# Two load queues, a reordered first stage and a longer warm-up in a two-layer mixer trunk

## The chip, the cores and the metric

The kernel runs on 1 core of one Trainium2 chip. The metric is device time in microseconds for one execution, as the median of the runs. Engines are named as in the profile: PE is TensorE's matmuls, PEld its weight loads, DVE is VectorE, ACT is ScalarE, POOL is GpSimd, SP issues DMAs.

## The reference

Two layers, each with one norm, one wide projection, four head groups and one output projection; a last norm ends it. x is 512 tokens by 1024, float32.

```python
def hybrid_layer(x, norm_w, w_in, w_out, ...):
    h = rmsnorm(x, norm_w)                 # x * rsqrt(mean(x^2) + eps) * norm_w
    p = split_cols(h @ w_in)               # 1024 by 3380 columns for four mixers
    o_a = dsa_mixer(...)   # indexer, top-128 keys of each query, attention
    o_b = nsa_mixer(...)   # compressed, selected and window attention, gated
    o_c = shortconv_mixer(...)
    o_d = pool_mixer(...)
    mixed = concat([silu(gate) * o for each group])
    return x + mixed @ w_out
```

## The kernel before

Tokens lie in four tiles of 128 (`NT`), the model width in eight chunks of 128 (`KC`). Each float32 factor of a projection is held as two float32r parts, high and low, and a product is three matmuls: L137 high by high, L138 low weights, L139 low activations, over eight chunks (24 matmuls of 360 columns for a tile of the first group).

`load_w` loads a group of columns of `w_in` by four quarters of its rows (two chunks each), casts a quarter to `wh` (for the first group on VectorE, L120) and subtracts to get `wl` (`lo`, L95; for the first group quarters 0 and 2 on GpSimd, 1 and 3 on VectorE). `first_loads(h)` puts the other first loads between these quarters. All DMAs of the first stage are issued by SP; at most eight are under way, since the ninth waits for the first one's landing.

The norm of a tile (`norm_tile`) works on two halves of 512 columns: ScalarE squares and sums (`junk`, L222), GpSimd adds the halves and takes the power -1/2 (L223, L234), VectorE multiplies x by the scale and by the norm's weights `g` (L237, `xn`), TensorE transposes four blocks (L246), ScalarE copies the high part of `hT` out of PSUM (L248), VectorE writes the low part (L95 `hT`). A tile's first matmul, L137, needs the high part; L139 needs the low part. After the 24 matmuls of a tile come the copies and the rotation of queries and keys, and four transposes (L385 and L386).

`g` is the norm's weight row, the same on all 128 partitions. Before the first norm TensorE runs 28 transposes of the identity on nothing (`WARM`). A scheduler fixes the order of instructions on each engine at build time; engines take their instructions in that order and wait on semaphores.

Of the kernel before, what the change touches and what calls it, by code (L numbers as in the profile page):

```python
# [17 lines left out]
P = 128  # L18
T = 512
# [8 lines left out]
TOPK = 128  # L28
BIG = 10  # places for tiles of [P, T]
WARM = 28  # products on nothing at the start  # L30
NEG = -1.0e30
MARK = -3.0e38
EPS = 1.0e-6

# first columns of the parts of w_in
A_Q, A_V, A_QI, A_KI, A_GATE, B_Q, B_KC, B_KS, B_GATE, C_B, C_GATE = 0, 320, 384, 640, 680, 936, 1192, 1320, 1588, 1844, 2612

# columns of the table of shape constants
TB64, TB32, TBC, TBN, TBW, TBL = 0, 128, 192, 224, 256, 258
# [26 lines left out]
def trunk(ctx: ExitStack, tc: tile.TileContext, x, norm_w, w_in, w_out, conv_w, pe_cmp, w_cmp_k, w_cmp_v,  # L66
# [26 lines left out]
    def lo(eng, dst, src, hi):  # L93
        """dst = src - hi, the part of src that its rounding to float32r left out."""
        eng.tensor_sub(dst, src, f(hi))  # L95

# [1 line left out]
    def load_w(src, segs, early=None, start=False):  # L98
        """segs: (first column, columns) runs of src that make up one group; by quarters of its rows.
        early: tag of a place that is still free for the loads; start: the first group of all"""  # L100
        n = sum(c for _, c in segs)
        parts = []
        stage = res.tile([P, KC, 384], F32, name=nm("ws"), tag=early) if early else None
        for h in range(4):
            if early:
                st = stage[:, 2 * h : 2 * h + 2, :]
            else:
                st = wp.tile([P, 2, 384], F32, name=nm("st"), tag="st", bufs=4)
            o = 0
            for c0, c in segs:  # L110
                nc.sync.dma_start(
                    st[:, :, o : o + c],
                    src[h * 256 : (h + 1) * 256, c0 : c0 + c].rearrange("(k p) c -> p k c", p=P))
                o += c
            if start:
                first_loads(h)
            wh = wp.tile([P, 2, 384], F32R, name=nm("wh"), tag="wh", bufs=6)
            wl = wp.tile([P, 2, 384], F32R, name=nm("wl"), tag="wl", bufs=6)
            if start:
                V.tensor_copy(wh[:, :, :n], st[:, :, :n])  # L120
            else:
                S.activation(wh[:, :, :n], st[:, :, :n], AF.Copy)  # L122
            lo(V if start and h % 2 else G, wl[:, :, :n], st[:, :, :n], wh[:, :, :n])
            parts.append((wh, wl))
        return parts
# [3 lines left out]
    def lin_tok(ps, act, i, w, c0, n, order=range(KC)):  # L129
        """ps[:, :n] = act (tokens of tile i) @ w[:, c0:c0+n]"""  # L130
        ts = slice(i * P, (i + 1) * P)
        order = list(order)
        for k in order:
            wh, wl = w[k // 2]
            rh, rl = wh[:, k % 2, c0 : c0 + n], wl[:, k % 2, c0 : c0 + n]
            st, sp = k == order[0], k == order[-1]
            PE.matmul(ps[:, :n], act[0][:, k, ts], rh, start=st, stop=False)  # L137
            PE.matmul(ps[:, :n], act[0][:, k, ts], rl, start=False, stop=False)  # L138
            PE.matmul(ps[:, :n], act[1][:, k, ts], rh, start=False, stop=sp)  # L139

    def lin_ch(act, w, c0):
        """(w[:, c0:c0+128])^T @ act^T : 128 channels by all tokens"""
        ps = bank("mm", 2)
        for k in range(KC):
            wh, wl = w[k // 2]
            lh, ll = wh[:, k % 2, c0 : c0 + P], wl[:, k % 2, c0 : c0 + P]
            PE.matmul(ps, lh, act[0][:, k, :], start=k == 0, stop=False)  # L147
            PE.matmul(ps, lh, act[1][:, k, :], start=False, stop=False)  # L148
            PE.matmul(ps, ll, act[0][:, k, :], start=False, stop=k == KC - 1)  # L149
        return ps  # L150

# [1 line left out]
    def half(b):  # L153
# [5 lines left out]
    def load_x(xt, src, i):  # L159
        for b in range(2):  # L160
            nc.sync.dma_start(xt[b], src[i * P : (i + 1) * P, half(b)])
# [7 lines left out]
    xt0 = [x_tile() for _ in range(NT)]  # L169
    load_x(xt0[0], x, 0)  # L170
    g_first = load_g(nc.sync, norm_w[0:1, :])
    ident = const.tile([P, P], F32, name="ident")
    make_identity(nc, ident)
    # the tensor engine's clock rises only after some microseconds of work: done on nothing while the loads run
    idle = bank("ms", 1)
    for _ in range(WARM):
        PE.transpose(idle[:, :P], ident, ident)
    tab = const.tile([P, TBL], F32, name="tab")
    mask = const.tile([P, T], F32, name="mask")
# [11 lines left out]
    def first_loads(h):  # L191
        """the other loads, between those of the first group of weights"""
        if h:
            load_x(xt0[h], x, h)
        if h == 1:
            nc.sync.dma_start(tab, table)
        if h == 3:
            G.memset(mask, 0.0)
# [19 lines left out]
    def mean_sq(xp, acc):  # L218
        """acc (EPS to begin with) and the part of the mean of squares that the columns xp make up"""
        junk = wk.tile([P, T], BF16, name=nm("junk"), tag="acc", bufs=3)  # L220
# [8 lines left out]
    def rms(xt, g, ms=None):  # L229
        """xt, g: by halves of the columns; ms: mean of xt's squares"""  # L230
        if ms is None:
# [20 lines left out]
    def rope(eng, z, n, half, tb, rows=P):  # L252
        """z: [rows, n, d], rotated in place; tb: [rows, 4*half] = cos, cos, -sin, sin"""
        r = 2 * half
# [12 lines left out]
    def pipeline(tasks, depth=4):  # L267
        """Starts a task with each round, and takes each of those under way a step further."""
        active = []
# [16 lines left out]
    def layer(l, hT, w_first, norm):  # L286
        """hT: the layer's normalized input, transposed, w_first: its first group of weights; norm, if any, writes
        the tiles of hT. Returns the like for the next layer."""
        xsrc = x if l == 0 else x1d
# [5 lines left out]

# [1 line left out]
        kiT = res.tile([P, T], F32R, name=nm("kiT"), tag="kiT")  # L297
# [3 lines left out]
        def group_idx(i, w):  # L301
            """indexer queries of tile i, and the scores of its tokens against those before"""
            ps = bank("mm", 2)
# [6 lines left out]
            yield  # L310
            # rows of qiT[h % 4]: high, high, low part of the queries; of kiT: high, low, high part of the keys
            pq = bank("tr", 2)
# [31 lines left out]

# [1 line left out]
        qT = {}  # L346
        kTA = [res.tile([P, T], F32R, name=nm("kTA"), tag=f"kTA{s}") for s in range(2)]
        vA = res.tile([P, NT, P], F32R, name=nm("vA"), tag="vA")
        # keys of the selected and of the window branch; the compressed ones stand before the latter
        kTB = [res.tile([P, 2, 32 + T], F32R, name=nm("kTB"), tag=f"kTB{s}") for s in range(2)]  # L350
# [3 lines left out]
        def stack_q(m, i, pq):  # L354
            """pq: two heads a transpose; even heads as (high, low), odd ones as (low, high) rows"""
            q = wk.tile([P, NH, P], F32R, name=nm("q" + m), tag="q" + m, bufs=NT)
# [60 lines left out]
        def group_bq(i, w):  # L417
            """queries of the second mixer, values of the first"""
            ps = bank("mm", 2)
# [13 lines left out]

# [1 line left out]
        kcT = [kTB[s][:, 1, 0:32] for s in range(2)]  # L435
# [47 lines left out]

# [1 line left out]
        sg = {}  # L485

        def gates(m, j, w, c0):
            """tanh form of silu, twice its value: x (1 + tanh(x / 2))"""
            ps = lin_ch(hT, w, c0)
# [5 lines left out]
        def probs(m, i, kT, bias, gcol, cmp=None):  # L495
            """softmax over the keys of tiles 0..i; cmp: takes the scores of the 32 compressed keys, which stand
            before the others in kT"""
            n = P * (i + 1)
            c = 32 if cmp else 0
            per = T // n if n <= T // 2 else 1  # heads to a tile  # L500
            per = min(per, 2)
# [35 lines left out]
        def finish(m, i, po, c0):  # L537
            """adds the two halves of po, gates, and splits the result into the mixed activations"""
            ob = wk.tile([HD, T], F32, name=nm("ob"), tag="rl", bufs=2)
# [58 lines left out]

# [1 line left out]
        def cd(s="cd"):  # L600
# [63 lines left out]

# [1 line left out]
        def norm_a(i, w):  # L666
# [124 lines left out]
```

## Time and profile before

| | |
|---|---|
| median of 3 runs | 576.3 us (573.21, 576.3, 577.37) |
| profiled execution, span | 577.7 us, mean granted TensorE clock 0.971 |
| PE busy | 542.4 us, 94% of the span |
| VectorE, ScalarE, GpSimd busy | 448.9, 318.3, 296.0 us |
| DMA | 51.14 MB, mean 89 GB/s |

The profiled execution is one further execution. Its own time is given by its span, from the first to the last instruction, and is 1.4 us above the median of the runs. In the rows of a timeline the columns are start, duration, engine, line, operation, output and inputs by the program's names, and in brackets how long the engine stood idle ahead of it and what ended that. A row of a table by windows has the window, its length, then busy time of PE, PEld, DVE, ACT and POOL with counts, the granted clock, the DMA share and GB/s. A row of a group has a count, the busy time and the mean of one in ns.

### The profile page before, as it was taken

Reading aid. Unit: us, or ns where it says so; the run is one execution under the profiler, and the core shown is the slowest. Engines: PE = TensorE matmul, PEld = TensorE weight load, DVE = VectorE, ACT = ScalarE, POOL = GpSimd, SP = SyncE. Lnnn points to the kernel's source line nnn. Section 1 sums busy time; section 2 is a strip of 40 time slices with the busy share of each in tenths; the row PEclk is TensorE's granted clock in tenths of the full one; section 3 lists DMA queues with packets and bytes.
Section 4 is the critical chain, followed back from the end, with each engine's and each line's share of the span. In section 5 each row is a group of like instructions: output and inputs, shape, how many; then the busy total and the mean of one; then the engine's idle time right before and its main releaser. Section 6 shows DMA issues by size and latency. Waiting matters only on the chain.

```text
span 577.7 us, 9703 instructions
## 1 busy us (share of the span) xinstructions
PE 542.4 (94%) x3088; PEld 473.1 (82%) x3088; DVE 448.9 (78%) x1154; ACT 318.3 (55%) x787; POOL 296.0 (51%) x394
## 2 busy tenths in 40 slices
PE   5989799798999999999999989989999999999995
PEld 4989697676878877699999978768788887869895
DVE  4867899799999977762275769987999997897523
ACT  3457855253547566663455595536454756565433
POOL 4755641364546194643675455326554639273342
PEclk9899999799999999999999999987999999999999
DMA  8632311283222020526531512116513212123303
GB/s 260 192 94 54 74 34 23 56 209 83 54 56 65 28 79 13 147 91 198 147 117 48 141 35 64 37 37 178 134 30 81 64 48 58 52 88 114 111 1 145
DMA packets 70370, 51.14 MB, mean 89 GB/s; under 512 B 19248, under 2 KB 64432, under 8 KB 70320
## 3 DMA queue, kind: packets, MB, share of 16 engines
q1 hardware_dynamic: 70320, 50.54, 31.8%
q8 instruction: 24, 0.39, 0.3%
q14 instruction: 26, 0.21, 0.1%
HBM read 46.33 MB, written 4.19 MB: 87 GB/s over the span
## 4 chain that ended last, share of the span: by engine, by line
PE 67%; DVE 22%; ACT 4%; POOL 2%; issue 2%; DMA 2%; SPq 1%; POOLq 0%; ACTq 0%; DVEq 0%
PE mm L139 9%; PE mm L137 9%; PE mm L138 8%; PE mm L147 7%; PE mm L148 7%; PE mm L149 7%; PE tr L529 4%; DVE acc L342 4%; DVE acc L331 4%; DVE m L341 3%; PE ms L467 2%; PE s L509 2%; PE s L510 2%; PE pv L535 2%; PE pv L534 2%
## 5 line engine op out<-in xcount | busy, mean ns | idle before, releaser
L95 POOL TENSOR_TENSOR wl<-st,wh 128x768 fp32r<-128x768 f32 (+4 forms) x94 | 159.2, 1713 | 63.2 <-ACT wh L122 51.2
L147 PE MATMUL mm<-hT,wh 128*128 128x512 f32 x272 | 110.1, 405 | 3.8 <-DVE sg L493 3.0
L149 PE MATMUL mm<-hT,wl 128*128 128x512 f32 x272 | 108.2, 399 | 0.0
L148 PE MATMUL mm<-hT,wh 128*128 128x512 f32 x272 | 108.1, 399 | 0.0
L522 POOL TENSOR_SCALAR pb<-pb,rs 128x512 f32<-128x512 f32 (+3 forms) x96 | 53.7, 577 | 98.8 <-DVE rs L519 39.0
L515 ACT ACTIVATE pb<-pb,mn 128x512 f32<-128x512 f32 (+3 forms) x96 | 53.7, 559 | 72.1 <-DVE mn L513 71.6
L122 ACT ACTIVATE wh<-st 128x768 fp32r<-128x768 f32 (+4 forms) x92 | 70.7, 775 | 25.4 <-DMA st<-in_w_in_dram 9.2
L137 PE MATMUL mm<-wh,hT 128*128 128x360 f32 (+3 forms) x240 | 74.8, 313 | 8.1 <-ACT hT L248 4.3
L139 PE MATMUL mm<-wh,hT 128*128 128x360 f32 (+3 forms) x240 | 74.7, 312 | 0.9 <-DVE hT L95 0.9
L138 PE MATMUL mm<-wl,hT 128*128 128x360 f32 (+3 forms) x240 | 74.1, 310 | 0.0
L147 PEld LDWEIGHTS mm<-hT,wh 128*128 128x128 f32 x272 | 51.8, 191 | 14.2 <-DVE sg L493 3.5
L137 PE MATMUL mm<-wh,mT 128*128 128x384 f32 (+1 forms) x192 | 61.7, 323 | 0.3 <-ACT mT L604 0.3
L139 PE MATMUL mm<-wh,mT 128*128 128x384 f32 (+1 forms) x192 | 61.1, 320 | 0.6 <-DVE mT L95 0.6
L138 PE MATMUL mm<-wl,mT 128*128 128x384 f32 (+1 forms) x192 | 61.4, 320 | 0.0
L148 PEld LDWEIGHTS mm<-hT,wh 128*128 128x128 f32 x272 | 51.9, 191 | 9.7 <-issue 0.4
L149 PEld LDWEIGHTS mm<-hT,wl 128*128 128x128 f32 x272 | 51.4, 189 | 10.1 <-issue 0.5
L95 DVE TENSOR_TENSOR pl<-tr,ph 128x512 fp32r<-128x512 f32 (+1 forms) x68 | 45.9, 681 | 15.3 <-ACT ph L532 14.0
L137 PEld LDWEIGHTS mm<-wh,hT 128*128 128x128 f32 x240 | 46.1, 193 | 9.7 <-ACT hT L248 4.8
L341 DVE MAX8 m<-acc 128x8 f32<-128x384 f32 (+2 forms) x96 | 52.1, 552 | 0.4
L342 DVE MATCH_REPLACE8 acc<-m,acc 128x384 f32<-128x384 f32 (+2 forms) x96 | 52.0, 543 | 0.1
L139 PEld LDWEIGHTS mm<-wh,hT 128*128 128x128 f32 x240 | 46.1, 192 | 1.7 <-DVE hT L95 1.7
L138 PEld LDWEIGHTS mm<-wl,hT 128*128 128x128 f32 x240 | 46.2, 193 | 0.2
(194 smaller groups left out, 1171.5 us busy)
## 6 DMA issues: line engine op xcount, KB each, us to landing
st<-in_w_in_dram SPq DMA_DIRECT2D x104, 128.0 KB, 2.8
st<-in_w_in_dram SPq DMA_DIRECT2D x28, 256.0 KB, 3.0
st<-in_w_out_dram SPq DMA_DIRECT2D x16, 384.0 KB, 3.3
x<-in_x_dram SPq DMA_DIRECT2D x16, 256.0 KB, 4.1
st<-in_w_in_dram SPq DMA_DIRECT2D x8, 320.0 KB, 4.8
st<-in_w_out_dram SPq DMA_DIRECT2D x8, 256.0 KB, 3.0
x1d<-x SPq DMA_DIRECT2D x8, 256.0 KB, 2.4
x<-x1d SPq DMA_DIRECT2D x8, 256.0 KB, 3.3
```

What stands on the lines that cost most here:

```text
L95: eng.tensor_sub(dst, src, f(hi))
L122: S.activation(wh[:, :, :n], st[:, :, :n], AF.Copy)
L137: PE.matmul(ps[:, :n], act[0][:, k, ts], rh, start=st, stop=False)
L138: PE.matmul(ps[:, :n], act[0][:, k, ts], rl, start=False, stop=False)
L139: PE.matmul(ps[:, :n], act[1][:, k, ts], rh, start=False, stop=sp)
L147: PE.matmul(ps, lh, act[0][:, k, :], start=k == 0, stop=False)
L148: PE.matmul(ps, lh, act[1][:, k, :], start=False, stop=False)
L149: PE.matmul(ps, ll, act[0][:, k, :], start=False, stop=k == KC - 1)
L341: V.max(m8, a)
L342: V.match_replace(a, m8, a, MARK)
L515: S.activation(p, p, AF.Exp, scale=-1.0, bias=mn[:, h : h + 1], accum_out=rs[:, h : h + 1])
L522: G.tensor_scalar(p, p, rs[:, h : h + 1], 0.0, op0=OP.mult, op1=OP.add)
```

## The change

Four edits, all ahead of the first layer's projections:

- x tile 0 and the norm's weights are loaded by ScalarE's queue, the weights as one row of 4 KB (`grow`) and not as two broadcasts of 256 KB to all partitions. SP starts at once with the first group of weights.
- x tiles 1 to 3 and the table come behind all four quarters of that group, not between them.
- `g_first` now lies in two banks of PSUM: TensorE multiplies a row of ones by `grow`, which writes the row to all partitions. `xn` of the first norm reads it from there.
- 44 transposes instead of 28.

```diff
-WARM = 28
+WARM = 44
...
-    load_x(xt0[0], x, 0)
-    g_first = load_g(nc.sync, norm_w[0:1, :])
+    grow = wk.tile([1, DM], F32, name="grow", tag="om", bufs=1)
+    for b in range(2):
+        S.dma_start(xt0[0][b], x[0:P, half(b)])
+    S.dma_start(grow, norm_w[0:1, :])
+    ones = const.tile([1, P], F32, name="ones")
+    G.memset(ones, 1.0)
...
     for _ in range(WARM):
         PE.transpose(idle[:, :P], ident, ident)
+    g_first = [bank("s", 2) for _ in range(2)]
+    for b in range(2):
+        PE.matmul(g_first[b], ones, grow[:, half(b)], start=True, stop=True)
...
     def first_loads(h):
-        if h:
-            load_x(xt0[h], x, h)
-        if h == 1:
-            nc.sync.dma_start(tab, table)
         if h == 3:
+            load_x(xt0[1], x, 1)
+            nc.sync.dma_start(tab, table)
+            load_x(xt0[2], x, 2)
+            load_x(xt0[3], x, 3)
             G.memset(mask, 0.0)
```

The rest of the diff takes comments away. Lines of the changed kernel behind this place are 8 higher (L237 is L245 there).

The scheduler orders the first stage anew. VectorE's first rows before: `xn_193` and `xn_194` are the halves of tile 0, 245 and 246 those of tile 1; `wh_140`, 150, 159 and 172 are the quarters of the weights.

```order
L237 SCALAR_TENSOR_TENSOR xn_193<-x_75,ss_189,g_85 128x512
L237 SCALAR_TENSOR_TENSOR xn_194<-x_76,ss_189,g_86 128x512
L120 CAST wh_140<-st_137 128x2x360
L120 CAST wh_150<-st_144 128x2x360
L95 TENSOR_TENSOR wl_151<-st_144,wh_150 128x2x360
L95 TENSOR_TENSOR hT_136<-tr_197,hT_135 128x4x128
L120 CAST wh_159<-st_154 128x2x360
L95 TENSOR_TENSOR hT_136<-tr_204,hT_135 128x4x128
L237 SCALAR_TENSOR_TENSOR xn_245<-x_77,ss_241,g_85 128x512
L237 SCALAR_TENSOR_TENSOR xn_246<-x_78,ss_241,g_86 128x512
L120 CAST wh_172<-st_163 128x2x360
```

The same place after the change, from the second cast to the first low part of `hT`: `xn_213` and 214 are tile 0, 265 and 266 tile 1, 337 and 338 tile 2; `s_139` and `s_140` are the norm's weights in PSUM.

```order
L120 CAST wh_167<-st_164 128x2x360
L95 TENSOR_TENSOR wl_168<-st_164,wh_167 128x2x360
L120 CAST wh_174<-st_171 128x2x360
L120 CAST wh_192<-st_178 128x2x360
L95 TENSOR_TENSOR wl_193<-st_178,wh_192 128x2x360
L245 SCALAR_TENSOR_TENSOR xn_213<-x_75,ss_209,s_139 128x512
L245 SCALAR_TENSOR_TENSOR xn_265<-x_77,ss_261,s_139 128x512
L245 SCALAR_TENSOR_TENSOR xn_214<-x_76,ss_209,s_140 128x512
L245 SCALAR_TENSOR_TENSOR xn_266<-x_78,ss_261,s_140 128x512
L245 SCALAR_TENSOR_TENSOR xn_337<-x_79,ss_333,s_139 128x512
L245 SCALAR_TENSOR_TENSOR xn_338<-x_80,ss_333,s_140 128x512
L95 TENSOR_TENSOR hT_156<-tr_217,hT_155 128x4x128
```

The first row for tile 0's `hT` stood behind two `xn` and now stands behind six, and all four casts stand ahead of the first `xn`.

ScalarE's first rows before; `x_75` and 76 are the halves of tile 0, 77 and 78 of tile 1.

```order
L222 ACTIVATE junk_184,ss_185<-x_75 128x512
L222 ACTIVATE junk_188,ss_189<-x_76 128x512
L222 ACTIVATE junk_236,ss_237<-x_77 128x512
L248 ACTIVATE hT_135<-tr_197 128x4x128
L222 ACTIVATE junk_240,ss_241<-x_78 128x512
L248 ACTIVATE hT_135<-tr_204 128x4x128
```

And after, with its three DMA issues; `x_79` and 80 are tile 2, 81 and 82 tile 3.

```order
L172 DMA x_75<-in_x_dram 128x512
L172 DMA x_76<-in_x_dram 128x512
L173 DMA grow<-in_norm_w_dram 1x1024
L230 ACT_TABLE_LOAD
L230 ACTIVATE junk_204,ss_205<-x_75 128x512
L230 ACTIVATE junk_208,ss_209<-x_76 128x512
L230 ACTIVATE junk_256,ss_257<-x_77 128x512
L230 ACTIVATE junk_260,ss_261<-x_78 128x512
L230 ACTIVATE junk_328,ss_329<-x_79 128x512
L230 ACTIVATE junk_332,ss_333<-x_80 128x512
L230 ACTIVATE junk_415,ss_416<-x_81 128x512
L256 ACTIVATE hT_155<-tr_217 128x4x128
```

The copy of tile 0's `hT` stood behind three squares and now stands behind seven, so behind the load of tile 3's first half. Behind the transposes of tile 2 (L385, L386) the order of all engines is the same in both kernels.

More of the change, by code (lines that the diff above doesn't have):

```diff
@@ L191, in first_loads @@
     def first_loads(h):
-        if h:
-            load_x(xt0[h], x, h)
-        if h == 1:
+        if h == 3:
+            load_x(xt0[1], x, 1)
             nc.sync.dma_start(tab, table)
-        if h == 3:
+            load_x(xt0[2], x, 2)
+            load_x(xt0[3], x, 3)
             G.memset(mask, 0.0)
```

## The prediction

> **What bounds the kernel now.** I read the page first (busy shares, the chain that ended last), then the first 40 us of the timeline engine by engine, since every edit lies there.
>
> ```profile
> PE 542.4 (94%) x3088; PEld 473.1 (82%) x3088; DVE 448.9 (78%) x1154; ACT 318.3 (55%) x787; POOL 296.0 (51%) x394
> PE 67%; DVE 22%; ACT 4%; POOL 2%; issue 2%; DMA 2%; SPq 1%; POOLq 0%; ACTq 0%; DVEq 0%
> ```
>
> TensorE sets the time of nearly the whole span; DMA holds 2% of the chain, 11 us, and those stand at the start and at the final norm's weights. So the change is worth what it moves TensorE in the first stage. As a landmark I take the pair of transposes L385/L386 of token tile 2: all that the change reorders lies ahead of it, and behind it all engines run the same rows.
>
> ```profile
> 12.49 0.67 PE L137 MATMUL mm<-wh,hT 128*128 128x360 f32 x1 [2.96 <-ACT hT L248]
> 13.71 0.67 PE L139 MATMUL mm<-wh,hT 128*128 128x360 f32 x1 [0.26 <-DVE hT L95]
> 26.71 0.43 PE L139 MATMUL mm<-wh,hT 128*128 128x360 f32 x1 [0.64 <-DVE hT L95]
> 32.80 0.43 PE L137 MATMUL mm<-wh,hT 128*128 128x360 f32 x1 [1.32 <-ACT hT L248]
> 39.49 0.27 PE L386 MATMUL tr<-ident,kk 128*128 128x128 f32 x1
> ...
> 12.20:19.10 6.90, 6.36 (x21) 5.82 (x22) 5.86 (x8) 3.57 (x10) 4.97 (x6) 0.51 1.06 353
> 19.10:26.00 6.90, 6.90 (x47) 6.60 (x45) 6.67 (x11) 3.76 (x11) 5.46 (x7) 1.00 0.61 154
> ```
>
> Dense work begins with L139 at 13.71 and reaches the landmark at 39.49, 25.8 us later. Two waits lie between, 0.64 + 1.32 = 1.96. And the granted clock (third number from the end of the last two rows) was 0.51 until 19.1 and 1.00 after: 5.4 us of dense work at half speed, which cost 2.7. What is left, 21.1 us, is work that the change does not touch.
>
> **Loads.** The change removes two 256 KB broadcasts of `norm_w`, adds 4 KB (`grow`), sends tile 0 of x through ScalarE's queue and puts all four quarters of weights ahead of x tiles 1 to 3.
>
> ```profile
> 0.80 0.87 SPq L161 DMA_DIRECT2D x<-in_x_dram  x2
> 3.53 0.63 ACT L222 ACTIVATE junk<-x 128x512 bf16<-128x512 f32 x1 [1.45 <-DMA x<-in_x_dram]
> ...
> GB/s 0 0 0 177 376 311 123 140 180 260 326 342 345 354 357 351 327 326 252 310 350 309 369 347 377 341 369 355 358 348 347 361 360 363 366 332 159 69 28 3
> x<-in_x_dram SPq DMA_DIRECT2D x8, 256.0 KB, 4.4
> st<-in_w_in_dram SPq DMA_DIRECT2D x4, 320.0 KB, 5.7
> g<-in_norm_w_dram SPq DMA_DIRECT2D x2, 256.0 KB, 5.6
> st<-in_w_in_dram SPq DMA_DIRECT2D x4, 40.0 KB, 5.4
> ```
>
> The GB/s row has 40 slices of 0.6 us. Bytes flow from 2.1 us; right behind tile 0 stand three slices at 123 to 180, the broadcasts, and then the stream runs at about 340. Now tile 0 (0.52 MB) and all weights (4 x 360 KB, 1.47 MB) come first: 2.0 MB at 340 is 5.9 us, so all have passed at 8.0 and count as landed at about 8.5 (the first piece of x passed at 2.9 and its reader started at 3.53). Quarter 0 and tile 0 together, 0.9 MB, land near 5.2, quarters 1 and 2 near 6.3 and 7.4. Tile 1 follows at 10.0, the table and tile 2 at 11.9, the halves of tile 3 at 12.7 and 13.5.
>
> A rule speaks against a larger gain here. The Trainium skill, DMA: Bandwidth & Descriptors, section "Issuing engines are not separate DMA queues", says that transfers started by different engines share the same 16 DMA engines, and only issue time is saved. In the trace one queue alone keeps 309 to 377 GB/s in nearly every slice from 6.6 to 21 us, which agrees; if two queues did add up, by the same sum the weights would land near 5.5 and the total be up to 3 us better.
>
> **Norm weights and warm-up.** Neither is on the path. The two spreading matmuls read float32 512 columns wide, as L661 does, and 16 more transposes run at the faster spacing:
>
> ```profile
> L661 PE MATMUL ms<-cd,pw x8: 592/612/697, 219.7 to 514.1; 128*128 128x512 f32 x8
> 1.88 4.98 PE L177 MATMUL ms<-ident 128*128 128x128 f32 x28 [1.88 <-POOL ident masks.py:199]
> L177 PE MATMUL ms<-ident x28: 272/418/473, 1.9 to 6.6; 128*128 128x128 f32 x28
> ```
>
> Durations fall from 418 to 272 ns in the group, and starts from 0.21 to 0.11 us apart; 16 more take 1.7 us and end at 8.6, the matmuls at 9.6. Their reader, the first `xn`, cannot start before 10.6 (below), so the cover is the weights' splitting; without it they would cost up to 2.6. ScalarE's three DMA issues, at SP's 0.43 us each, delay its table load (1.28 us, from 0.79 before) to end at 3.4, before tile 0 lands.
>
> **The new chain on VectorE.** Here the order counts. VectorE now casts all four quarters first, then runs six of the eight `xn` across tiles 0, 1 and 2, and only then writes the first low part of hT, for which L139 waits. The prices:
>
> ```profile
> 9.41 0.53 DVE L120 CAST wh<-st 128x720 fp32r<-128x720 f32 x1 [0.59 <-DMA st<-in_w_in_dram]
> 10.02 1.70 POOL L95 TENSOR_TENSOR wl<-st,wh 128x720 fp32r<-128x720 f32 x1 [3.91 <-DVE wh L120]
> 10.56 1.55 DVE L120 CAST wh<-st 128x720 fp32r<-128x720 f32 x1 [0.62 <-DMA st<-in_w_in_dram]
> 12.15 0.91 DVE L95 TENSOR_TENSOR wl<-st,wh 128x720 fp32r<-128x720 f32 x1
> L237 DVE SCALAR_TENSOR_TENSOR xn<-x,ss,g 128x512 f32<-128x512 f32 x16 | 17.0, 1091 | 13.9 <-DMA g<-in_norm_w_dram 7.2 <-POOL ss L234 6.6
> L493 DVE SCALAR_TENSOR_TENSOR sg<-sg,mm 128x512 f32<-128x512 f32 x8 | 5.5, 682 | 0.1
> L95 DVE TENSOR_TENSOR hT<-tr,hT 128x512 fp32r<-128x512 f32 x16 | 10.9, 685 | 3.9 <-ACT hT L248 3.7
> 4.34 0.19 POOL L223 TENSOR_SCALAR ss<-ss 128x1 f32<-128x1 f32 x1 [0.69 <-ACT junk L222]
> 5.21 0.26 POOL L223 TENSOR_SCALAR ss<-ss,ss 128x1 f32<-128x1 f32 x1 [0.68 <-ACT junk L222]
> 5.55 0.56 POOL L234 TENSOR_TENSOR ss<-ss,mhalf 128x1 f32<-128x1 f32 x1
> 29.53 0.20 POOL L216 TENSOR_SCALAR psh<-psc 128x4 f32<-128x4 f32 x1 [0.88 <-DMA psc<-in_pool_scale_dram]
> ```
>
> The second cast took 1.55 instead of 0.53 beside GpSimd's subtraction and ended 0.4 after it. Operations with one operand in PSUM (L493, L95 hT) kept 0.68, so `xn` with its weights in PSUM should take 0.68, not the mean 1.09.
>
> Step by step: cast 0 5.2 to 5.7; GpSimd's low part of quarter 0 until 7.5; cast 1, held as before, until 7.9; low part 1 until 8.7; casts 2 and 3 until 9.8; low part 3 until 10.6; `xn` of tile 0's first half until 11.2. The next is tile 1's first half, which waits for tile 1's scale. On GpSimd that scale stands behind the low part of quarter 2 (1.70). If GpSimd takes it at 9.3, it ends at 11.0 but holds VectorE's cast 3; if VectorE goes first, it runs 10.6 to 12.3. Two small operations and the power follow, 1.1 us: 12.1 or 13.4. Then five `xn` (1a, 0b, 1b, 2a, 2b), 3.2 us, and the low part, 0.7. L139 starts between 16.1 (the first case without VectorE's delay) and 17.4; the first case with it gives 16.9. I take 16.8, 3.1 later than 13.71. ScalarE adds nothing: its copy of tile 0 now waits for tile 3's first square (12.7 + 0.75), yet is done by 14.2, before VectorE asks for it.
>
> What comes back: by 17.4 the tiles 1 and 2 and half of 3 are normalized, and all weights split, so the 0.64 goes; at tile 3 both transposes stand together and TensorE waits for one copy of about 0.6 instead of 1.32. That is -1.4 (all of it: -1.96).
>
> One wait moves: GpSimd's two scalings of constants (L215, L216) now stand ahead of the rope of tile 0's queries. L216 waits for a load that landed at 29.5 and, with the queue ahead of it 3.7 shorter, lands near 25.8; the rope's four operations end near 27.1, ahead of their reader, L385 of tile 0, which ran at 28.5 and will run near 30. Without the earlier load it would cost 0.8.
>
> **The clock.**
>
> ```profile
> 5.40:12.20 6.80, 2.77 (x21) 2.06 (x19) 3.65 (x5) 1.08 (x3) 2.59 (x4) 1.00 0.98 323
> 8.03 0.66 PE L246 MATMUL tr<-ident,xn 128*128 128x128 f32 x4 [1.17 <-DVE xn L237]
> 8.87 0.66 PE L246 MATMUL tr<-ident,xn 128*128 128x128 f32 x4 [0.18 <-DVE xn L237]
> 28.47 0.49 PE L385 MATMUL tr<-ident,z 128*128 128x128 f32 x3
> ```
>
> It fell at 12.2, 5.4 us after the transposes ended at 6.86, though eight transposes ran in between; it rose 5.4 us after dense work began. Now the fill ends at 9.6, and four transposes near 11.3, two matmuls near 14 and four transposes near 14.5 are all until 16.8. I take the same 2.7 us lost: term 0, bounds -2.7 (never falls) and +4.3 (below). The Trainium skill, TensorE: Matmul & The Clock Gate, section "What's actually happening", has a free-running window of about 3.4 us, one idle window throttles and one busy one releases; by it the loss varies with the window's phase by up to 1.7 us and has the same mean before and after, so the sum stays. Its section "Part 4: PE-mode transpose" says that transposes do not count as busy; the trace disagrees, since durations fell to 272 ns while only transposes ran.
>
> **Sum**: +3.1 - 1.4 + 0 = +1.7 us. The landmark comes at 41.2, and the profiled execution's span of 577.7 would be 579.4. That span is 1.4 above the median of the runs, 576.3, inside their spread (573.21 to 577.37); on the median's footing I predict 578.0. Bounds of the sum, each term at its end: L139 at 14.7 (rival 2), all waits gone, clock up gives -3.7; 17.4, -0.7 for the waits, late clock gives +7.3.
>
> **Rivals.** (1) The longer fill keeps the clock up: 1.7 - 2.7 = -1.0, 575.3. For it: the fill reaches 9.6 instead of 6.86. Against: the stretch to 16.8 is longer than the one that let it fall, and as thinly filled.
>
> (2) VectorE and GpSimd do not hold each other up, and tile 1's scale is there in time: VectorE's own work after the last quarter's landing is 0.53 + 0.82 + 6 x 0.68 + 0.7 = 6.1, L139 at about 14.7, +1.0 - 1.96 = -1.0, 575.3. Against: the cast at 10.56. The Trainium skill, SBUF — State Buffer, section "Who interferes with whom", has them share one port pair which the first to start keeps for its whole instruction; the 1.55 us agrees.
>
> (3) The slower side: tile 0 and the weights, with rows of different lengths on two queues, run at the broadcasts' upper rate. 2.0 MB at 180 GB/s takes 11.1 us, weights at 13.7, 5.2 later, and VectorE's chain hangs on them: +6.9, 583.2. It decides from about 200 GB/s down. For it: the stream has dropped to 123 once. Against: the mixed rows of 320 and 40 KB loads ran at 340.
>
> (4) The gate opens late, as it did once:
>
> ```profile
> 384.00:398.00 14.00, 13.87 (x80) 11.87 (x81) 8.95 (x28) 5.78 (x13) 6.36 (x6) 0.51 0.48 121
> ```
>
> 14 us at half speed cost 7.0 against 2.7: +1.7 + 4.3 = +6.0, 582.3.
>
> **How the numbers follow.** Forecast 0.60, rival (1) 0.13, (2) 0.10, (3) 0.09, (4) 0.08. A measurement of this kernel can tell about 1%, 5.8 us, from no change. Slower by more needs over 582.1: most of (3) and half of (4), and the upper edge of the forecast, 0.18. Faster by more needs under 570.5, which no case reaches (both good rivals at once give 572.6); 0.09 is left for what the first stage's trace cannot show and for the 4 us between runs. 0.73 is between. The range, 572.8 to 582.7, holds the forecast, (1), (2) and (4).
>
> **What would show it.** Right: first `xn` near 10.6 behind the last low part; L139 at 16 to 17.5, later than before, though all weights landed by about 9; `xn` near 0.68; clock half again until 20 to 24; the landmark between 40 and 42. Wrong: L139 before 14, a clock of 1.00 through 12 to 20, weights later than 11, or a landmark within 1 us of 39.5 with a changed total, which would put the cause behind the first stage.

## The result: the first stage starts 4.5 us later, the total moves by 0.4%

The changed kernel took 579.36 us (median of 20 runs, 575.1 to 581.43), the kernel before 576.24 on the same chip (20 runs, 572.54 to 578.95). The ratio is 1.0042, 95% interval 1.0022 to 1.0063: 2.4 us more, from 1.3 to 3.6. The forecast was 578.0 with 572.8 to 582.7.

The page of the changed kernel's profiled execution says nothing new: TensorE still sets the time.

```profile
PE 545.3 (95%) x3108; PEld 476.7 (83%) x3108; DVE 442.2 (77%) x1154; ACT 318.6 (55%) x787; POOL 295.1 (51%) x395
PE 66%; DVE 19%; ACT 5%; POOL 4%; issue 3%; DMA 2%; SPq 0%; POOLq 0%; ACTq 0%; DVEq 0%
```

The timeline of the first stage shows where the time went. These are VectorE's and GpSimd's rows, in order of time, from the first weights to the low part that L139 waits for.

```profile
6.23 0.54 DVE L120 CAST wh<-st 128x720 fp32r<-128x720 f32 x1 [6.23 <-DMA st<-in_w_in_dram]
6.86 1.71 POOL L95 TENSOR_TENSOR wl<-st,wh 128x720 fp32r<-128x720 f32 x1 [1.36 <-DVE wh L120]
7.43 1.53 DVE L120 CAST wh<-st 128x720 fp32r<-128x720 f32 x1 [0.66 <-DMA st<-in_w_in_dram]
8.99 0.91 DVE L95 TENSOR_TENSOR wl<-st,wh 128x720 fp32r<-128x720 f32 x1
9.82 0.97 DVE L120 CAST wh<-st 128x720 fp32r<-128x720 f32 x2
10.42 1.92 POOL L95 TENSOR_TENSOR wl<-st,wh 128x720 fp32r<-128x720 f32 x1
10.82 2.29 DVE L95 TENSOR_TENSOR wl<-st,wh 128x720 fp32r<-128x720 f32 x1
13.04 0.73 DVE L245 SCALAR_TENSOR_TENSOR xn<-x,ss,s 128x512 f32<-128x512 f32 x1
14.20 3.38 DVE L245 SCALAR_TENSOR_TENSOR xn<-x,ss,s 128x512 f32<-128x512 f32 x5 [0.43 <-POOL ss L242]
17.50 0.69 DVE L95 TENSOR_TENSOR hT<-tr,hT 128x512 fp32r<-128x512 f32 x1
```

All weights are cast by 10.8, but the first `xn` starts at 13.04 (7.22 before), behind all four quarters; five more `xn` stand ahead of the low part. TensorE's rows in the same stretch: the spreading matmuls, the dense start, the only wait that is left, and the landmark.

```profile
9.61 1.98 PE L185 MATMUL s<-grow,ones 1*128 1x512 f32 x4
18.24 0.67 PE L139 MATMUL mm<-wh,hT 128*128 128x360 f32 x1 [0.86 <-DVE hT L95]
36.22 0.43 PE L137 MATMUL mm<-wh,hT 128*128 128x360 f32 x1 [0.35 <-ACT hT L256]
42.48 0.27 PE L394 MATMUL tr<-ident,kk 128*128 128x128 f32 x1
...
14.20:24.40 10.20, 8.37 (x31) 7.43 (x30) 5.91 (x9) 3.92 (x9) 4.48 (x8) 0.50 0.71 192
```

L139 starts 4.5 later, the landmark 3.0 later. The last row is of the table by windows: the granted clock was 0.50 from 14.2 to 24.4.

One warning on single executions. This profiled one has a span of 574.5, shorter than the 577.7 of the kernel before, though the medians say the opposite. Both traces keep about the landmark's distance until 67 us (3.2 us there); then it changes, most where only one of them is at half clock (107.8 to 118.1 in the one before; 75.6 to 79.0, 331.6 to 335.0 and 345.2 to 348.6 in the other). GpSimd's third `u` still starts 3.5 us later in the changed kernel (108.84 against 105.31), VectorE's third `sg` 3.7 us earlier (128.97 against 132.64). Half speed for 10.2 us explains at most 5.1 of these 7.2 us; the rest is not explained. The stretches of half clock lie elsewhere in other executions too, as the table below shows for the first stage, so the first stage is read from profiles and the total from medians.

### The profile page after: what moved, and what is told of

The parts are those of the page before. It is cut to its first block, busy times and chain, and to the rows that moved or that the text cites. A ratio compares the mean times of both kernels' runs of the same rounds, so it can differ in the third digit from the quotient of the medians.

```text
span 574.5 us, 9737 instructions
## 1 busy us (share of the span) xinstructions
PE 545.3 (95%) x3108; PEld 476.7 (83%) x3108; DVE 442.2 (77%) x1154; ACT 318.6 (55%) x787; POOL 295.1 (51%) x395
## 4 chain that ended last, share of the span: by engine, by line
PE 66%; DVE 19%; ACT 5%; POOL 4%; issue 3%; DMA 2%; SPq 0%; POOLq 0%; ACTq 0%; DVEq 0%
PE mm L137 9%; PE mm L139 9%; PE mm L138 9%; PE mm L147 7%; PE mm L149 7%; PE mm L148 7%; PE tr L537 4%; DVE acc L350 3%; DVE m L349 3%; DVE acc L339 3%; PE s L517 2%; POOL wl L95 2%; PE s L518 2%; PE pv L542 2%; PE pv L543 2%
## 5 line engine op out<-in xcount | busy, mean ns | idle before, releaser
L137 PE MATMUL mm<-wh,hT 128*128 128x360 f32 (+3 forms) x240 | 76.7, 321 | 3.6 <-ACT gt L411 2.6
L139 PE MATMUL mm<-wh,hT 128*128 128x360 f32 (+3 forms) x240 | 76.8, 320 | 0.9 <-DVE hT L95 0.9
L138 PE MATMUL mm<-wl,hT 128*128 128x360 f32 (+3 forms) x240 | 76.0, 317 | 0.0
L139 PE MATMUL mm<-wh,mT 128*128 128x384 f32 (+1 forms) x192 | 61.1, 320 | 0.7 <-DVE mT L95 0.7
L138 PE MATMUL mm<-wl,mT 128*128 128x384 f32 (+1 forms) x192 | 61.4, 320 | 0.0
L137 PEld LDWEIGHTS mm<-wh,hT 128*128 128x128 f32 x240 | 48.1, 201 | 4.9 <-ACT gt L411 3.4
L139 PEld LDWEIGHTS mm<-wh,hT 128*128 128x128 f32 x240 | 47.9, 200 | 1.3 <-DVE hT L95 1.3
L138 PEld LDWEIGHTS mm<-wl,hT 128*128 128x128 f32 x240 | 48.1, 201 | 0.2
```

## The experiments

All were compared with the kernel before on the same chip, in five rounds. "Dense start" is the first L139 (the first matmul with a low part; L141 where lines were added). "Landmark" is the one of the prediction. The half clock ends at another moment in each execution. The column of the landmark therefore also gives it less lost clock: half of the time at half clock between the dense start and the landmark is taken off.

| kernel | first xn | dense start | half clock ends | landmark, and less lost clock | ratio to before, 95% |
|---|---|---|---|---|---|
| before | 7.22 | 13.71 | 19.1 | 39.49, 36.8 | 1 |
| the change | 13.04 | 18.24 | 24.4 | 42.48, 39.4 | 1.0042 (1.0022 to 1.0063) |
| 1 low part first | 12.96 | 15.86 | 18.0 | 39.21, 38.2 | 1.0031 (0.9997 to 1.0065) |
| 7 the same again | 12.79 | 16.15 | 16.8 | 39.28, 39.0 | 1.0020 (0.9996 to 1.0045) |
| 2 one queue | 13.31 | 18.50 | 21.4 | 41.13, 39.7 | 1.0040 (1.0010 to 1.0070) |
| 3 spreading alone | 11.38 | 15.19 | 17.7 | 38.13, 36.9 | 1.0004 (0.9978 to 1.0031) |
| 4 weights ahead alone | 6.58 | 14.07 | 19.9 | 39.38, 36.5 | 1.0038 (1.0011 to 1.0066) |
| 8 the same again | 6.44 | 14.21 | 18.9 | 39.02, 36.7 | 1.0012 (0.9992 to 1.0032) |
| 5 warm-up alone | 7.26 | 17.34 | 23.5 | 41.51, 38.4 | 1.0010 (0.9983 to 1.0036) |
| 6 order written out | 7.10 | 12.89 | 13.4 | 41.90, 41.7 | 1.0081 (1.0054 to 1.0107) |
| 9 row spread early | 6.67 | 10.55 | 12.5; again 26.2 to 29.6 | 41.25, 38.6 | 1.0029 (1.0006 to 1.0053) |
| 10 full rows | 7.18 | 11.31 | 8.9; again 26.0 to 29.4 | 41.69, 40.0 | 1.0047 (1.0017 to 1.0076) |
| 11 full rows, chain | 6.56 | 10.61 | 8.2 | other order | 0.9948 (0.9927 to 0.9969) |
| 12 one row, chain | 6.69 | 10.51 | 9.8; again 16.6 to 20.0 | other order | 0.9930 (0.9898 to 0.9962) |

### 1 and 7: tile 0's low part ahead of the other norms

```diff
+            with tc.issue_after(low0):
+                if i > 1:
+                    with tc.issue_after(copy0):
+                        xn = rms(xt, g, ms)
...
```

`low0` and `copy0` are tile 0's last low part (VectorE) and last copy (ScalarE); `issue_after` puts what stands in it behind them on the same engine.

> The changed kernel with one thing different: VectorE does the norms of tiles 1 to 3 only behind tile 0's last low part, and ScalarE the squares of tiles 2 and 3 only behind its last copy of tile 0. Loads, spreading matmuls, warm-up and casts stay. Theory (the order of rows carries the loss, 2.1 us of it by the five xn and the seven squares ahead of the low part): first xn still at 13.0, low part at 15.3, L139 at 16.0 to 16.6 and not 18.24, landmark at 40.2 to 41.2 and not 42.48, total 1 to 2 us under the change. Rival A (the loads, quarter 0 landing at 6.2, carry it all) and rival B (TensorE's longer fill and the spreading matmuls carry it all, as a late or half clock): the order is worth nothing, L139 stays at 17.5 or later and the landmark within 0.5 of 42.5.

VectorE's rows now have the low part right behind tile 0's two `xn`, and TensorE's first L139 and landmark follow.

```profile
12.96 1.39 DVE L245 SCALAR_TENSOR_TENSOR xn<-x,ss,s 128x512 f32<-128x512 f32 x2
15.08 0.69 DVE L268 TENSOR_TENSOR hT<-tr,hT 128x512 fp32r<-128x512 f32 x1 [0.72 <-ACT hT L267]
15.86 0.63 PE L139 MATMUL mm<-wh,hT 128*128 128x360 f32 x1
39.21 0.27 PE L407 MATMUL tr<-ident,kk 128*128 128x128 f32 x1
```

The order of rows held L139 by 2.4 of the 4.5; rivals A and B, by which the order is worth nothing, are out for the dense start. The landmark came ahead of the 40.2 to 41.2 expected because the half clock ended at 18.0; less lost clock it is 38.2 against the change's 39.4. By the ratios the total is about 0.6 us under the change, not 1 to 2, and its interval is wide, so the kernel was run again:

> The kernel of the first experiment once more, since its interval (0.9997 to 1.0065) left open whether the total follows the landmark. If it does: with the landmark at a like loss of clock 1.2 us behind before's, ratio 1.000 to 1.003, under the change's 1.0042. If it does not: 1.0035 or more.

1.0020, as expected if the total follows; but the interval still overlaps the change's own. Shown is the dense start, not the total.

### 2: one queue

```diff
-        S.dma_start(xt0[0][b], x[0:P, half(b)])
-    S.dma_start(grow, norm_w[0:1, :])
+        nc.sync.dma_start(xt0[0][b], x[0:P, half(b)])
+    nc.sync.dma_start(grow, norm_w[0:1, :])
```

> The changed kernel with tile 0 of x and the 4 KB row sent through SP's queue ahead of the weights; VectorE's order of rows is the same as in the change. Rival A (two queues that start together hold up quarter 0): its cast starts near 5.2 and not 6.23, first xn near 12.0, L139 near 17.2, landmark near 41.4, total 1 us under the change. Theory (it is the order; the first xn hangs on the casts and on GpSimd's low parts, whichever queue brings the loads): the cast may come earlier, but L139 gains under 0.5 and the landmark stays within 0.5 of 42.5. If quarter 0 lands at 6.2 here too, the second queue is no cause at all, and my 5.2 was simply too early.

First cast and L139 of this kernel, then GB/s over the first 24 us (40 slices of 0.6), of this kernel and of the change:

```profile
6.50 0.53 DVE L120 CAST wh<-st 128x720 fp32r<-128x720 f32 x1 [6.50 <-DMA st<-in_w_in_dram]
18.50 0.67 PE L139 MATMUL mm<-wh,hT 128*128 128x360 f32 x1 [0.86 <-DVE hT L95]
GB/s 0 0 0 150 399 350 149 319 325 328 304 348 318 314 328 355 368 362 396 382 379 355 362 358 357 355 351 357 360 368 357 259 78 46 32 1 1 21 50 12
```

```profile
GB/s 0 0 0 141 165 243 375 404 339 341 304 308 302 314 307 338 349 349 372 359 376 393 377 367 365 348 349 352 361 366 365 334 151 39 22 2 1 26 30 28
```

In these two executions the first slices differ (165 and 243 on two queues, 399 and 350 on one), but both streams had moved about 0.8 MB by 4.8 us, and the cast of quarter 0 could start at 6.50 on one queue and at 6.23 on two. So the second queue is not what made it late; the landing at 5.2 was forecast too early. Both rows add up to 0.9 MB, tile 0 and quarter 0, by about 5.1 us and to 1.2 MB by 6.0, so by this estimate from the rows bytes of the later quarters passed before the last of quarter 0. Rival A is out by the cast and by L139. The landmark came 1.35 ahead of the change's, more than the theory's 0.5 and near rival A's 41.4, but the half clock ended at 21.4 and not at 24.4; less lost clock it is 0.3 behind the change's.

### 3, 4, 8 and 5: each part alone

Spreading matmuls alone (order of the loads, SP's queue and 28 transposes as before):

```diff
-    g_first = load_g(nc.sync, norm_w[0:1, :])
+    grow = wk.tile([1, DM], F32, name="grow", tag="om", bufs=1)
+    nc.sync.dma_start(grow, norm_w[0:1, :])
+    ones = const.tile([1, P], F32, name="ones")
+    G.memset(ones, 1.0)
...
+    for b in range(2):
+        PE.matmul(g_first[b], ones, grow[:, half(b)], start=True, stop=True)
```

> The kernel before with one part of the change: the norm's weights as a 4 KB row, spread by two matmuls behind 28 transposes. Loads on SP in the order of before. VectorE's order then has three casts and four xn (tiles 0 and 1 in turn) ahead of the first low part. Theory (the order is what costs): first xn near 11.2, L139 near 14.6, 0.9 later than 13.71, though tile 0, the row and quarter 0 all land earlier than before; landmark 39.5 to 40.5, total within 1 us of before. Rival B (the spreading matmuls themselves hold the first xn): they end behind 11 and the first xn follows them directly. Rival C (removing 0.5 MB of broadcasts is worth what the bytes take): L139 1 us or more ahead of 13.71, total 1 to 2 us under before.

The matmuls, the four `xn` that the scheduler put ahead of the low part, and L139:

```profile
7.91 1.98 PE L183 MATMUL s<-grow,ones 1*128 1x512 f32 x4
11.38 2.71 DVE L243 SCALAR_TENSOR_TENSOR xn<-x,ss,s 128x512 f32<-128x512 f32 x4
14.45 0.68 DVE L95 TENSOR_TENSOR hT<-tr,hT 128x512 fp32r<-128x512 f32 x1
```

The matmuls end at 9.9 and the first `xn` starts 1.5 later: rival B is out. L139 comes at 15.19, 0.6 later than the theory had it. The landmark, forecast at 39.5 to 40.5, came at 38.13, partly because the half clock ended early; less lost clock it equals that of before, as the total does. Rival C is out by L139, which it had at 12.7 or earlier; of its gain of 1 to 2 us in total, the interval leaves no more than 1.3.

Weights ahead alone:

```diff
-        if h:
-            load_x(xt0[h], x, h)
-        if h == 1:
-            nc.sync.dma_start(tab, table)
         if h == 3:
+            load_x(xt0[1], x, 1)
+            nc.sync.dma_start(tab, table)
+            load_x(xt0[2], x, 2)
+            load_x(xt0[3], x, 3)
```

> The kernel before with one part of the change: all four quarters of the weights ahead of tiles 1 to 3 of x, broadcasts and one queue as before. VectorE's order keeps both xn of tile 0 ahead of the casts and its low parts right behind the third and fourth cast. Theory (earlier weights are worth the waits of 0.64 and 1.32, as long as the order stays): first xn at 7.2, L139 at 13.0 to 13.8, landmark 38.3 to 39.3, total 0.5 to 1.5 us under before. Rival D (tiles 1 to 3 now come too late): L139 as before, but waits of over 2 us behind it for xn or hT of tile 1, landmark at 40 or later, total 1 us or more over before.

> The kernel with the weights ahead alone once more, on another day of runs: its landmark was before's (39.38 against 39.49), yet its ratio was 1.0038 (1.0011 to 1.0066). If the total follows the first stage: ratio 0.998 to 1.001, and the first value was chance of the clock's windows. If something behind the first stage costs 2 us wherever the weights are ahead of tiles 1 to 3: 1.003 to 1.005 again, and the trace shows what waits.

By the first run the part costs 2.2 us with a landmark like before's, where a gain of 0.5 to 1.5 was expected. The second gave 1.0012, between its two cases. What the profile shows agrees in both: L139 at 14.07 and 14.21, a little later than expected, no wait of 0.64 or 1.32 behind it, the landmark less lost clock 0.1 to 0.3 earlier. Rival D fell on the waits. Whether the part alone is worth a little or costs a little stays open.

44 transposes alone:

```diff
-WARM = 28
+WARM = 44
```

> The kernel before with one part of the change: 44 warm-up transposes and not 28. Loads and broadcasts as before; VectorE's order now has both xn of tile 1 ahead of tile 0's first low part. Theory (the longer fill costs nothing by itself, but the order that it brings does): fill ends near 8.6, first xn still at 7.2, xn of tile 1 at 14.5 as before, behind them the low part near 17.2 and L139 near 17.9, 4 later than 13.71; the waits of 0.64 and 1.32 mostly gone; landmark near 42 at the same lost clock, total 1 to 3 us over before. Rival E (the longer fill keeps the clock up and nothing else changes): no half clock ahead of 30, L139 within 0.5 of 13.71, total 1 to 3 us under before.

VectorE's `xn` of tile 1 and, behind them, tile 0's low parts; then L139 with the wait ahead of it, the landmark, and a row of the table by windows:

```profile
13.77 2.92 DVE L237 SCALAR_TENSOR_TENSOR xn<-x,ss,g 128x512 f32<-128x512 f32 x2
16.61 1.28 DVE L95 TENSOR_TENSOR hT<-tr,hT 128x512 fp32r<-128x512 f32 x2
17.34 0.67 PE L139 MATMUL mm<-wh,hT 128*128 128x360 f32 x1 [3.38 <-DVE hT L95]
41.51 0.27 PE L386 MATMUL tr<-ident,kk 128*128 128x128 f32 x1
13.40:23.60 10.20, 6.82 (x25) 6.21 (x25) 9.44 (x11) 4.72 (x12) 8.23 (x10) 0.51 0.95 287
```

A number that only sets idle transposes moved L139 by 3.6 us, because the scheduler then put tile 1's `xn` ahead of tile 0's low part. The clock fell all the same, so rival E is out. The total moved by 0.6 us only, under the 1 to 3 expected, and its interval holds no change.

### 6, 9 and 10: the order written out

In these the first group's loads stay ahead of tiles 1 to 3, on one queue, but the order of tile 0 is fixed by edges: cast 0, both `xn` of tile 0, low part of tile 0, low part of quarter 1, and so on; ScalarE casts quarter 2 (and in the sixth quarter 1).

```diff
+        c0 = V.tensor_copy(W(wh, 0), W(st, 0)).ins
+        last = c0
+        for b in range(2):
+            with tc.issue_after(last):
+                last = V.scalar_tensor_tensor(y[b], xt[b], ms, g_first[b], ...).ins
...
+        with tc.issue_after(last):
+            last = low(0)
```

> The loads of the change on one queue, the 4 KB row and spreading matmuls behind 12 transposes with 8 more after them, and the order of the first stage written out: VectorE casts quarter 0, then both xn of tile 0, tile 0's first low part, low part of quarter 1, tile 0's second low part, quarter 3, tile 1; ScalarE casts quarters 1 and 2 and copies tile 0 between them; tiles 2 and 3 behind tile 1. Theory (the earlier loads are worth what the order lets through): first xn at 7.0 to 8.0, L139 at 9.8 to 11.0, waits inside tile 0 under 1.5 in all, landmark at 33 to 36.5, total 3 to 6 us under before, ratio 0.990 to 0.996. Rival F (the total does not follow the first stage, as the weights ahead alone made 578.6 with a landmark like before's): landmark as said, total within 1 us of before or over it. Rival G (the loads or the casts hold it anyway): L139 at 12.5 or later, total within 1 us of before.

TensorE's rows of the sixth: the spreading at half speed, the dense start, three new waits, the landmark.

```profile
4.91 3.78 PE L188 MATMUL s<-grow,ones 1*128 1x512 f32 x4
18.48 0.63 PE L371 MATMUL tr<-ident,xn 128*128 128x128 f32 x4 [1.89 <-DVE xn L366]
27.08 0.43 PE L139 MATMUL mm<-wh,hT 128*128 128x360 f32 x1 [1.73 <-ACT hT L262]
34.04 0.63 PE L260 MATMUL tr<-ident,xn 128*128 128x128 f32 x4 [1.90 <-DVE xn L251]
41.90 0.27 PE L482 MATMUL tr<-ident,kk 128*128 128x128 f32 x1
```

580.37 us, 4.7 over before by the ratio, though the dense start came 0.8 ahead of before's. The theory is out. Rival G was right on the start alone. Rival F's words on the total would cover it, but not its landmark, which came at 41.90 and not at 33 to 36.5. Moving the spreading matmuls ahead of the clock's rise nearly doubled them (3.78 against 1.98), and then TensorE waited for tiles 1 to 3. The ninth and tenth mend the start. `WARM` counts the transposes ahead of and behind the spreading matmuls; the row goes by ScalarE's queue, and VectorE casts quarter 1:

```diff
-WARM = (12, 8)
+WARM = (4, 5)
-    nc.sync.dma_start(grow, norm_w[0:1, :])
+    S.dma_start(grow, norm_w[0:1, :])
-        c1 = S.activation(W(wh, 1), W(st, 1), AF.Copy).ins
...
+            last = V.tensor_copy(W(wh, 1), W(st, 1)).ins
```

The tenth differs from the ninth in this:

```diff
-    grow = wk.tile([1, DM], F32, name="grow", tag="om", bufs=1)
+    grow = wk.tile([P, DM], F32, name="grow", tag="om", bufs=1)
+    V.memset(grow, 0.0)
-    S.dma_start(grow, norm_w[0:1, :])
+    S.dma_start(grow[0:1, :], norm_w[0:1, :])
-    ones = const.tile([1, P], F32, name="ones")
-    G.memset(ones, 1.0)
+    ones = const.tile([P, P], F32, name="ones")
+    V.memset(ones, 1.0)
```

> The order of the sixth experiment once more, mended where it lost: the 4 KB row alone on ScalarE's queue, the spreading matmuls behind 4 transposes, 5 more transposes behind them, and VectorE casts quarter 1 so that ScalarE's first copies are free. The matmuls still have one row of weights. In the sixth experiment TensorE worked from 2.2 to 12.3, 3.78 of it in the two one-row matmuls, and the granted clock still rose only at 13.39. Theory H (a matmul with one row of weights does not count for the clock, transposes over 128 rows do): the clock rises at 10 or later again, the spreading takes 3.5 to 3.8, L139 at 9.8 to 11.0, landmark at 34.5 to 37.5. Theory I (any matmul counts, the sixth experiment had only bad luck with the windows): clock up by 5.6 to 9.1, landmark at 33 to 35. Total 2 to 5 us under before by either, if the total follows the landmark.

> The kernel before this one with one thing different: the row stands in a zeroed tile of 128 partitions and is multiplied by 128 x 128 ones, so that the two spreading matmuls have 128 rows of weights; the same columns, the same places in every queue. Theory H: the clock now rises at 5.6 to 9.1 (at most two windows of 3.41 us after the work begins) and is not lost before the landmark, L139 at 9.6 to 10.8, landmark 1 to 3 us ahead of the one-row kernel's. Theory I: no difference in the clock between the two beyond where the windows happen to lie, landmarks within 1 us. The total is then 3 to 6 us under before, ratio 0.990 to 0.995.

TensorE in the ninth: spreading, transposes behind it, then the dense start.

```profile
3.21 3.78 PE L188 MATMUL s<-grow,ones 1*128 1x512 f32 x4
6.92 1.33 PE L191 MATMUL ms<-ident 128*128 128x128 f32 x5
10.55 0.63 PE L141 MATMUL mm<-wh,hT 128*128 128x360 f32 x1
```

And in the tenth, with the later wait for tile 1:

```profile
5.02 3.75 PE L189 MATMUL s<-grow,ones 128*128 128x512 f32 x4 [2.03 <-DMA grow<-in_norm_w_dram]
8.56 0.90 PE L192 MATMUL ms<-ident 128*128 128x128 f32 x5
11.31 0.43 PE L141 MATMUL mm<-wh,hT 128*128 128x360 f32 x1
16.70 0.63 PE L373 MATMUL tr<-ident,xn 128*128 128x128 f32 x4 [1.88 <-DVE xn L368]
```

On the rise of the clock theory H held: 0.63 for a matmul at 10.55 is half speed, 0.43 at 11.31 is full; in the granted clock's record the ninth rises at 12.5, the tenth at 8.9. That the clock then stays up until the landmark did not hold: in both it fell again at 26. On the time both theories failed: dense start 2.4 to 3.2 ahead of before's, landmark 1.8 to 2.2 behind it (the tenth's behind the ninth's), ratios of 1.0029 and 1.0047. The gain turned into new waits for tiles 1 to 3 (1.88 here for tile 1's `xn`); for tiles 2 and 3 the order within their norms was still left to the scheduler.

### 11 and 12: all four norms in one chain

```diff
+        for i in range(1, NT):
...
+                with tc.issue_after(last):
+                    last = V.scalar_tensor_tensor(y[b], xt0[i][b], ms, g_first[b], ...).ins
...
+                with tc.issue_after(last):
+                    last = V.tensor_sub(hT[1][:, k, ts], p, f(hT[0][:, k, ts])).ins
```

The transposes of a tile are put ahead of the last two chunks of the tile before.

> The tenth experiment with the norms of tiles 2 and 3 in one written order too: each tile's two xn behind the low parts of the tile before, its transposes ahead of the last two chunks of the tile before. In the sixth experiment TensorE stood 1.73 for tile 2's copy and 1.90 and 0.60 for tile 3's xn. Theory: those waits fall under 0.5 in all and the landmark comes another 2 to 3 us earlier than in the tenth, at 30 to 33; total 5 to 8 us under before, if the later stages, whose order the scheduler then writes a little differently, lose nothing. Rival: GpSimd and VectorE, which split the next group's weights at that time, are the limit: the waits come back elsewhere and the landmark moves by under 1.

> The eleventh experiment with the spreading matmuls back at one row of weights; the 4 KB row lands earlier (about 3.2 against 4.4), since nothing zeroes its tile first. It tells which of the two, written order or full rows, makes the eleventh faster than before. By theory H the clock rises at 10 to 13 and not at 8.3, TensorE does the first 12 to 20 matmuls of tile 0 at half speed, and since tile 1's xn sets the next wait (16.1 in the ninth, 16.3 in the eleventh) most of that is hidden: total within 1.5 us of the eleventh's 573.2, ratio 0.993 to 0.998. If the full rows carry the gain: ratio 1.000 or more.

TensorE's waits that are left in the eleventh, and its first matmul of the later group that waits for `gt`, which stood at 64.10 in the kernel before:

```profile
16.28 0.63 PE L375 MATMUL tr<-ident,xn 128*128 128x128 f32 x4 [2.16 <-DVE xn L370]
24.50 0.43 PE L139 MATMUL mm<-wh,hT 128*128 128x360 f32 x1 [1.35 <-ACT hT L379]
61.52 0.42 PE L139 MATMUL mm<-wh,hT 128*128 128x320 f32 x1 [0.79 <-ACT gt L503]
```

```profile
64.10 0.41 PE L137 MATMUL mm<-wh,hT 128*128 128x320 f32 x1 [1.03 <-ACT gt L403]
```

In the twelfth, with one row of weights in the spreading matmuls:

```profile
3.21 3.78 PE L188 MATMUL s<-grow,ones 1*128 1x512 f32 x4
6.92 1.33 PE L191 MATMUL ms<-ident 128*128 128x128 f32 x5
62.71 0.42 PE L139 MATMUL mm<-wh,hT 128*128 128x320 f32 x1 [0.78 <-ACT gt L502]
```

Both beat both kernels: 573.18 us (576.7 for before on its chip) and 572.39 (575.88). The waits for tile 3 are gone; those for tiles 1 and 2 are not (2.16 and 1.35 in the eleventh), and the gain of 3 to 4 us by the ratios is under the 5 to 8 that I expected of the eleventh. Full rows are not needed for it: the twelfth has one row and is as fast. Its clock rose at 9.8, ahead of the dense start and a little ahead of theory H's 10 to 13.

Where the gain lies is not shown. At the row above the two kernels are 2.6 and 1.4 us earlier than the kernel before, which lost 2.7 us of clock on the way; the eleventh lost none behind its dense start and the twelfth 1.7. Less lost clock the row stands at 61.4 before, 61.5 and 61.0: up to here the two profiles gained clock, and at most 0.4 us of waits. Over all runs, though, the mean granted clock is 0.972 in these two kernels and 0.972 to 0.973 in the kernel before. And in these two alone the scheduler wrote the rows of all compute engines in another order up to about 250 us; in experiments 1 to 10 all engines run the rows behind the landmark as before. No run has the written order of the first stage with the later rows as before, so whether the gain comes from the one or the other stays open.

## Why the prediction was right or wrong

**What held.** The sign, the size of the total (1.7 forecast, 2.4 measured with 1.3 to 3.6) and the mechanism in the first stage: weights earlier, L139 later, because VectorE does all casts and six `xn` ahead of the low part. `xn` from PSUM took 3.38 for five, 0.68 each, as forecast. The waits gave back 1.96 - 0.35 = 1.6 (forecast 1.4). The clock fell at 14.1 and cost 6.1 us of dense work at half speed, 3.1 against 2.7 (forecast: the same). Sum: 4.5 - 1.6 + 0.4 = 3.3; measured at the landmark 3.0.

**What was mis-sized: the first term.** L139 came at 18.24 against 16.8, outside its bounds of 16.1 to 17.4. With it the first `xn` (13.04, not near 10.6) and the landmark (42.48, not 40 to 42) missed the signs that the prediction had named. Three steps were off, and that one of them was off the other way, so that no more than 1.4 was left, is luck:

- Quarter 0 was to land near 5.2 and its cast started at 6.23: +1.0. I had let 0.9 MB pass in their order at 340 GB/s. The slow start explains about 0.3 of it, as 0.9 MB had passed by 5.1 and not by 4.8; the rest, by the estimate of experiment 2, is bytes of later quarters that passed ahead of them. On one queue it was no earlier.
- Low part 3 was to take 0.82 behind the casts; it took 2.29, beside GpSimd's low part of quarter 2 (10.42 to 12.34): +1.5. I had seen the second cast held in the same way and applied it to casts alone. The Trainium skill, SBUF — State Buffer, section "Who interferes with whom", says that a VectorE instruction with two inputs in SBUF contends with GpSimd's reads; 2.29 here against 0.91 for the same operation at 8.99 agrees.
- Tile 1's scale was to hold VectorE until 12.1 or 13.4, 0.9 or more behind the first `xn`; it held it for 0.43 only. From the first `xn` to L139 it was 5.2 us and not 6.2: -1.0.

The spreading matmuls were mis-sized too (1.98 for the two, ending at 11.6 and not 9.6), without effect: the first `xn` starts at 13.04.

**The rivals.** (1) The longer fill did not keep the clock up, in the change or alone (experiment 5). (2) VectorE and GpSimd did hold each other up. (3) The two queues did not run at 180 GB/s beyond the first slices; all quarters were cast by 10.8. (4) The full clock came back 6.1 us after the dense start, not 14. The moved wait for L216's constant (L224 here) ended at 27.3 rather than 25.8, still ahead of its reader.

**What the total does with it.** For the whole change the landmark less lost clock moved by 2.6 us and the total by 2.4. In experiments 1 to 10 the same difference lies within the interval of the ratio in each run, save the first run of experiment 4 (-0.3 against 0.6 to 3.8); the largest is that of experiment 6, 4.9 at the landmark and 3.1 to 6.2 in total. That the order costs the time is shown for the dense start (experiments 1, 5 and 7); for the total the intervals are too wide to show it part by part.

The clock's term rests on one execution of each kernel. Over the 20 runs of the change the mean granted clock was 0.969, over the 105 of the kernel before in the experiments' rounds 0.972, by estimate 3.6 us more at half clock, worth at most 1.8 of the 2.4. In the two profiles 2.6 us of additional half clock lie ahead of the dense start, where TensorE waits anyway. So how the total divides between order and clock is not shown.

## What to carry to other kernels

Where a scheduler fixes the order, any edit of the first stage, even a count of idle instructions, is an edit of the order on every engine: read the new rows of the engine that is waited for before pricing the loads. An earlier start pays only if every tile behind it is fed as early: experiments 9 and 10 started 2 to 3 us earlier and ended later. With the order of all four tiles written out the same loads won 0.5 to 0.7%, but the rows behind the first stage came out in another order too: when a written order wins, look whether it is the written rows that won. A total that moves by less than its runs spread (up to 9 us here) wants a landmark in the trace and a second run.

## What the hardware showed beyond that

A matmul with one row of weights does not seem to count for the clock. The record of the granted clock has its first entry when it rises, so ahead of that durations tell: in the twelfth experiment the one-row matmuls filled 3.21 to 6.99, and the five transposes behind them still ran slowly (1.33 against 0.90 in the tenth). The record rises at 13.4, 12.5 and 9.8 in the three kernels that spread one row early (sixth, ninth, twelfth), 7.6 us or more after TensorE began at 2.16, and in that time TensorE did not pause. It rises at 8.9 and 8.2 in the two with 128 rows (tenth, eleventh), 3.9 and 3.8 us after those matmuls began. The Trainium skill, TensorE: Matmul & The Clock Gate, section "What's actually happening", lets one busy window of about 3.4 us release the clock. The half-clock stretches of the first stage here last one, two or three times 3.4, which agrees. But the window from 3.0 to 6.4 in the twelfth, counted back from its rise, held 0.3 us of transposes and then one-row matmuls without a pause, and released nothing; there the measurement differs from the rule. Row counts between 1 and 128 were not tried. The total did not gain from full rows: in the eleventh and in the twelfth TensorE next stands 2.16 us for tile 1's `xn`, until 16.28 and 16.40.
